# Three rows of an adaLN modulation: from accumulating blocks on VectorE to row products that are summed along the row

## The chip, the cores and the metric

The kernel runs on one core of one Trainium2 chip. What counts is the device time of one execution, in microseconds (us). The kernel before takes 1460.43 us in the median of three runs (1458.61 to 1460.6).

## The reference

One layer of a hybrid diffusion backbone on 256 latent and 256 context tokens of width 2048, everything in float32. Cut to what matters here:

```python
m = silu(c) @ w_mod + b_mod                       # c: 2048 numbers, w_mod: 2048 x 12288
sh1, sc1, g1, sh2, sc2, g2 = split(m, 6)          # six rows of 2048, each (shift, scale, gate) twice
hx = rmsnorm(x, norm1_g) * (1 + sc1) + sh1        # the context tokens go the same way with silu(c_ctx)
z  = hx @ w_in + b_in                             # 2048 x 5648
s5, conv, mlstm = three mixers of z               # state-space scan, convolution, attention-like mLSTM
x  = x + g1 * (concat(s5, conv, mlstm) @ w_out)
hx2 = rmsnorm(x, norm2_g) * (1 + sc2) + sh2
x  = x + g2 * ((silu(hx2 @ wg) * (hx2 @ wu)) @ w_ffn_out)     # inner width 5632
out = rmsnorm(x, norm_f_g)
```

The first two modulation rows (sh1, sc1) are made at the start. The other four, called rows 0 to 3 here (g1, sh2, sc2, g2), are made while the mixers run. g1 is needed in the output projection, sh2 and sc2 behind it at the second norm, and g2 only in the second matrix of the feed-forward.

## The kernel before

Activations lie transposed: 128 features on the partitions, tokens along the free dimension. Every large weight is split into two parts, `whi` and `wlo`, each of a type that TensorE multiplies fast. The weights come as 386 chunks of 128 x 1024, that is eight 128 x 128 tiles, in the order in which TensorE wants them. For each chunk SyncE starts the load into `raw` (`raw_dma`), ScalarE writes `whi` (a cast, L201) and VectorE writes `wlo = raw - whi` (L168). `raw`, `whi` and `wlo` have three buffers each. TensorE (PE) then multiplies with `whi` and `wlo` (L208). So PE can't begin a chunk before VectorE (DVE) has written its `wlo`.

The stages on PE, one after the other: the input projection (first the parts for S5, convolution and keys, then values, queries and the output gate), the gated unit of S5, the output projection in two halves of 16 chunks, then the feed-forward in four blocks. Beside them run jobs: Python generators that the function `pump` steps along by a running estimate of the time on PE (`sc.pe`). These are the convolution (`conv_job`, tile `XB` on DVE), the S5 scan (`s5_job`, tiles `Vr`, `U`, `tmp`), the attention heads (tiles `RH`, `qh`, `dn`) and `mod_job`, which makes the modulation rows 0 to 3. The program that this writes is then put in order once more by the framework's scheduler, for each engine; an instruction that `keep_in_program_order` names keeps its place. Engines work off their queues in order.

`mod_job` before, lines 726 to 764: the weights of the four rows come as 128 loads of 512 KB into four buffers `wm`, which POOL issues (L337, `mod_dma`); a load waits until its buffer has been read. Row 0 is a matrix-vector product on PE, in four column blocks. Rows 1 to 3 are made on DVE: of a block of 512 columns it takes 16 pieces of 128 x 512 and adds up `macc = piece * silu(c) + macc`, with silu(c) as a number for each partition. The first of the 16 is a scaled copy on ScalarE (ACT), the other 15 are `SCALAR_TENSOR_TENSOR` on DVE (L179). The 128 partial sums of each column lie on the partitions then, so PE transposes the block in four pieces (L755) and ACT adds each along the free dimension (L761, a pass and a read of the accumulator). A call `need_mod(q)` steps the job until row q is done: `need_mod(0)` before the output projection, `need_mod(2)` between its halves, `need_mod(3)` before the second matrix of the feed-forward. Row 3 may start only when `go` is 3, which is set in the first block of the feed-forward; the first ACT instruction of each of its blocks keeps its program order.

Of the kernel before, what the change touches and what calls it, by code (L numbers as in the profile page):

```python
# [10 lines left out]
F32 = mybir.dt.float32  # L11
# [8 lines left out]
KT = 16  # L20
# [12 lines left out]
MV_LEAD = 8  # L33
WMQ = 62
MOD_PACE = 3200.0
MOD_PACE_F = 4000.0
MOD_PACE_D = 5000.0
P_CONV, P_S5, P_MOD, P_ATT, P_GATE = (3, 3, 2, 4, 1)
AHEAD, LAG = 3500.0, 500.0
PUMP_EVERY = 8  # L40
# [2 lines left out]
CONV_STEP = 2  # L43
GO_AT = {'k': 2}
LEAD_R, LEAD_S = 2, 1
MOD_PE = {(0, b) for b in range(4)}

# [98 lines left out]


@with_exitstack  # L150
def hybrid_layer_kernel(ctx: ExitStack, tc: tile.TileContext, xt, ctxt, wm1, wmr, wst, wg, bvrow, pvd, cstd, s5p, out):
    nc = tc.nc
    V, S, P, G = nc.vector, nc.scalar, nc.tensor, nc.gpsimd
    sb = ctx.enter_context(tc.tile_pool(name="sb", bufs=1))
# [20 lines left out]
            V.tensor_scalar(o, a, s1, s2, op0=op0, op1=op1)  # L175
        sc.dve += 62 + 0.6 * n_of(o)

    def stt(o, a, s, b, op0, op1):
        V.scalar_tensor_tensor(o, a, s, b, op0=op0, op1=op1)  # L179
        sc.dve += 62 + 1.05 * n_of(o)  # L180

    def vcopy(o, a):
# [11 lines left out]
    def act(o, a, f, bias=0.0, scale=1.0, pin=False):  # L194
        i = S.activation(o, a, f, bias=bias, scale=scale)  # L195
        if pin:
            tc.keep_in_program_order(i)
        sc.act += 190 + 0.84 * n_of(o)
# [24 lines left out]
    def bbank():  # L223
        return bank("b", 3)
# [106 lines left out]
    def wm_dma(key, src, q=None):  # L331
        slot = (4 * key[0] + key[1]) % NWX if len(key) == 2 else 0
        if slot < NWM:
            wm[key] = sb.tile([128, 1024], F32, name="wm", tag="wm", bufs=NWM)
        else:
            wm[key] = wm_extra[slot - NWM]
        i = (q or nc.gpsimd).dma_start(wm[key], src)  # L337
        if q is not None:
            tc.keep_in_program_order(i)
# [33 lines left out]

    plan_pump()

    cs = sb.tile([128, KT, 32], F32, name="cs")
    V.memset(cs, 0.0)
    act(cs[:, :, 0], pvc("c", 0, 16), AF.Silu)
    act(cs[:, :, 1], pvc("cc", 0, 16), AF.Silu)
    b1sc = sb.tile([128, 16], F32, name="b1sc")  # L380
    ts(b1sc, pvc("bm", 16, 16), 1.0, OP.add)

    hx = sb.tile([128, KT, 2, NT], F32R, name="hx", tag="hx")
# [326 lines left out]

    mods = sb.tile([128, 4, 16], F32, name="mods")

    mq = [(q, b, kp) for q in range(4) for b in range(4) for kp in range(8)]
    mst = {"d": 0, "q": 0, "go": 0}

    def phase(n):
# [2 lines left out]
    def mod_dma():  # L719
        if mst["d"] < len(mq):  # L720
            i = mq[mst["d"]]
            wm_dma(i, wmr[i[0], i[1], i[2]])
            mst["d"] += 1

    def mod_job():
      for q in range(4):
        while mst["go"] < q:
            yield 500
        for b in range(4):
            on_pe = (q, b) in MOD_PE  # L730
            acc = sb.tile([128, 512], F32, name="macc", tag="macc", bufs=1)
            if on_pe:
                psm = bbank()
            for kp in range(0, 8, 2):
                w = [wm.pop((q, b, kp + i)).rearrange("p (k n) -> p k n", k=2) for i in range(2)]
                for j in range(4):
                    kt = 2 * kp + j
                    wj = w[j // 2][:, j % 2, :]
                    s = cs[:, kt, 0:1]
                    if on_pe:  # L740
                        mm(psm[32 * j:32 * j + 32, :], cs[:, kt, :], wj, kt < 4, kt >= 12, native=True, tp=(0, 32 * j),
                           pin=j > 0)
                    elif kt == 0:
                        act(acc, wj, AF.Copy, scale=s, pin=q == 3)
                    else:
                        stt(acc, wj, s, acc, OP.mult, OP.add)
                mod_dma()
                mod_dma()
                yield 2 * (MOD_PACE if on_pe else MOD_PACE_D if q < 3 else MOD_PACE_F)
            dst = mods[:, q, 4 * b:4 * b + 4]  # L750
            if on_pe:
                acopy(acc, psm)
            ps = bbank()
            for j in range(4):
                P.transpose(ps[:, 128 * j:128 * j + 128], acc[:, 128 * j:128 * j + 128], ident)  # L755
                sc.pe += 110
            if on_pe:
                rsum(dst, ps.rearrange("p (f j r) -> p f j r", f=4, j=4)[:, :, :, 0])
            else:
                for j in range(4):  # L760
                    S.activation(acc[:, 128 * j:128 * j + 128], ps[:, 128 * j:128 * j + 128], AF.Copy,  # L761
                                    accum_out=dst[:, j:j + 1])
                    sc.act += 390
            tt(dst, dst, pvc("bm", 32 + 16 * q + 4 * b, 4), OP.add)
            yield
        mst["q"] = q + 1

    def need_mod(q):
        mst["go"] = max(mst["go"], q)
# [550 lines left out]
def pack(inp):  # L1320
    f = {k: np.asarray(v) for k, v in inp.items()}

    def cols(v):
        return np.ascontiguousarray(v.reshape(-1, 128).T)

    def feat(x):
        return np.ascontiguousarray(x.T.reshape(KT, 128, NT).transpose(1, 0, 2))

    a = {}
    a["xt"] = feat(f["x"][0])  # L1330
    a["ctxt"] = feat(f["ctx"][0])
    wmod = f["w_mod"][0]
    m1 = wmod[:, :4096].reshape(4, 4, 128, 2, KT, 128)
    a["wm1"] = np.ascontiguousarray(m1.transpose(4, 0, 2, 1, 3, 5)).reshape(KT, 4, 128, 1024)
    mr = wmod[:, 4096:].reshape(8, 2, 128, 4, 4, 512)
    a["wmr"] = np.ascontiguousarray(mr.transpose(3, 4, 0, 2, 1, 5)).reshape(4, 4, 8, 128, 1024)
    mats = {"in": f["w_in"][0][:, :OFF_G], "out": f["w_out"][0], "glu": f["s5_w_glu"][0], "ffi": f["w_ffn_in"][0],
            "ffo": f["w_ffn_out"][0]}
    til = {k: m.reshape(m.shape[0] // 128, 128, m.shape[1] // 128, 128) for k, m in mats.items()}
    w = np.empty((NCH, 128, CH, 128), np.float32)  # L1340
    for i, (m, kt, ct) in enumerate(ORDER):
        w[i // CH, :, i % CH, :] = til[m][kt, :, ct, :]
    a["wst"] = w.reshape(NCH, 128, CH * 128)
    gi = np.array([0, 1, 2, 3, 8, 9, 10, 11, 4, 5, 6, 7, 12, 13, 14, 15])
    g = f["w_in"][0][:, OFF_G:][:, gi]
    a["wg"] = np.ascontiguousarray(g.reshape(KT, 128, 16).transpose(1, 0, 2))
    bi = f["b_in"][0]
    a["bvrow"] = np.ascontiguousarray(bi[None, OFF_V:OFF_O])
    pv = np.zeros((128, NPV + 96), np.float32)

    def put(name, m):
        o, wd = PV[name]
        assert m.shape == (128, wd), (name, m.shape)
        pv[:, o:o + wd] = m

    put("c", cols(f["c"][0]))
    put("cc", cols(f["c_ctx"]))
    put("n1g", cols(f["norm1_g"][0]))
    put("bm", cols(f["b_mod"][0]))
    put("n2g", cols(f["norm2_g"][0]))  # L1360
    put("nfg", cols(f["norm_f_g"]))
    put("bs5", cols(bi[:512]))
    put("bcv", cols(bi[OFF_CONV:OFF_Q]))
    put("bq", cols(bi[OFF_Q:OFF_K]))
    put("bk", cols(bi[OFF_K:OFF_V]))
    put("bo", cols(bi[OFF_O:OFF_G]))
    dw = f["conv_dw_w"][0]
# [12 lines left out]
    put("dcol", np.tile(f["s5_d"][0].reshape(16, 32).T, (4, 1)))  # L1380
    bg = np.zeros((128, 1), np.float32)
    for r in range(4):
        bg[32 * r:32 * r + 4, 0] = bi[OFF_G:][gi[4 * r:4 * r + 4]]
    put("bg", bg)
    a["pvd"] = pv
    cst = np.zeros((128, NCST), np.float32)
    cst[:, C_ID:C_ID + 128] = np.eye(128)
    cst[:, C_MF:C_MF + 128] = np.triu(np.ones((128, 128)))
    cst[:, C_MR:C_MR + 128] = np.tril(np.ones((128, 128)))
    for r in range(32):  # L1390
        q = r % 16
        cst[r, C_SELG + 32 * (q // 4) + q % 4] = 1.0
    cst[:, C_K:C_K + 128] = np.arange(128)
    a["cstd"] = cst
    sp = np.empty((16, 2, 4, 16, 128), np.float32)
    for i, nm in enumerate(("s5_b_re", "s5_b_im")):
        sp[:, :, i] = f[nm][0].reshape(2, 16, 128, 16).transpose(1, 0, 3, 2)
    for i, nm in enumerate(("s5_c_re", "s5_c_im")):
        sp[:, :, 2 + i] = f[nm][0].transpose(0, 1, 3, 2).reshape(2, 16, 128, 16).transpose(1, 0, 3, 2)
    a["s5p"] = np.ascontiguousarray(sp.transpose(0, 4, 1, 2, 3))  # L1400
    return a


_INS = ["xt", "ctxt", "wm1", "wmr", "wst", "wg", "bvrow", "pvd", "cstd", "s5p"]


# [19 lines left out]
```

## Time and profile before

| | |
|---|---|
| median of 3 runs | 1460.43 us |
| the profiled execution | 1461.92 us, of which the span from the first to the last instruction is 1460.2 us |
| PE busy | 1416.0 us, 97% of the span |
| DVE busy | 1058.8 us, 73% |
| ACT busy | 740.4 us, 51% |
| mean granted TensorE clock | 0.99 of full speed |

PE is busy nearly all the time. DVE's share is a mean over stages that differ much, so it has to be read for each stage: the view of windows does that. The view of lines and the timeline give what one instruction costs, and the chain that ended last tells on which instructions the end depends.

### The profile page before, as it was taken

To read this page: it belongs to the slowest core of one execution; us is meant where nothing else is said; L and a number is where in the kernel's file an instruction comes from. 1 tells how busy PE (TensorE), PEld (TensorE's weight loads), DVE (VectorE), ACT (ScalarE), POOL (GpSimd) and SP (SyncE) were. 2 spreads that over 40 slices of the span, in tenths; PEclk is the share of its full clock that TensorE was granted. 3 is DMA by queue.
4 is the path that set the end of the run, shared out by engine and by line. 5 is a ranking of instruction groups with operands and counts; after the bars stand their busy time and mean duration, and the time that the engine had idled before them with its cause. 6 is when DMAs were issued, how large, how long until landed. Compare 5 with 4: busy or idle time off the path is not lost.

```text
span 1460.2 us, 25526 instructions
## 1 busy us (share of the span) xinstructions
PE 1416.0 (97%) x9856; PEld 1242.3 (85%) x9856; DVE 1058.8 (73%) x2104; ACT 740.4 (51%) x1279; POOL 107.3 (7%) x207
## 2 busy tenths in 40 slices
PE   6999899999999999999999999999999999999996
PEld 3888787887878999898998888888888888888885
DVE  7655699998988887888877778566555665556665
ACT  4334786654656555645555545433444334444353
POOL 1221111110001010011000010000000000000000
PEclk9999999999999999999999999999999999999998
DMA  9998464443436666689478787555555555555553
GB/s 365 359 359 300 156 234 142 164 165 117 143 120 226 219 238 236 243 310 343 145 234 278 277 299 240 187 189 186 189 188 187 187 188 188 188 188 188 188 177 112
DMA packets 87929, 315.31 MB, mean 216 GB/s; under 512 B 10096, under 2 KB 10880, under 8 KB 87808
## 3 DMA queue, kind: packets, MB, share of 16 engines
q1 hardware_dynamic: 60912, 216.67, 43.4%
q0 software_dynamic: 26896, 97.02, 18.8%
q8 instruction: 77, 1.26, 0.3%
q14 instruction: 44, 0.36, 0.1%
HBM read 311.55 MB, written 2.10 MB: 215 GB/s over the span
## 4 chain that ended last, share of the span: by engine, by line
PE 87%; DVE 5%; ACT 3%; DMA 2%; issue 1%; SPq 0%; DVEq 0%; ACTq 0%
PE ps_m L208 55%; PE ps_qk L208 20%; PE ps_b L208 12%; DMA raw<-in_wst_dram 1%; DVE tmp L168 1%; ACT whi L201 1%; DVE macc L179 1%; DVE wlo L168 1%; DMA tmp<-in_wg_dram 1%; ACT tmp L195 1%; PE ps_b L845 0%; ACT U L201 0%; PE ps_b L755 0%; DVE tmp L191 0%; DVE tmp L179 0%
## 5 line engine op out<-in xcount | busy, mean ns | idle before, releaser
L168 DVE TENSOR_TENSOR wlo<-raw,whi 128x1024 fp32r<-128x1024 f32 x386 | 471.3, 1222 | 268.0 <-ACT whi L201 264.4
L201 ACT CAST whi<-raw 128x1024 fp32r<-128x1024 f32 x386 | 403.8, 1047 | 478.8 <-PE ps_m L208 240.6
L208 PE MATMUL ps_m<-h,whi 128*128 128x512 f32 (+1 forms) x800 | 251.9, 369 | 3.5 <-ACT h L195 3.5
L208 PE MATMUL ps_m<-ffa,whi 128*128 128x512 f32 x704 | 248.8, 395 | 0.0
L208 PE MATMUL ps_qk<-h,whi 128*128 128x512 f32 (+1 forms) x688 | 233.2, 383 | 0.0
L208 PE MATMUL ps_m<-h,wlo 128*128 128x256 f32 x704 | 199.6, 284 | 0.0
L208 PE MATMUL ps_m<-ffa,wlo 128*128 128x256 f32 x704 | 198.9, 283 | 0.0
L208 PE MATMUL ps_m<-hx,whi 128*128 128x256 f32 x960 | 187.2, 291 | 5.5 <-ACT hx L195 3.6
L208 PE MATMUL ps_qk<-h,wlo 128*128 128x256 f32 x656 | 185.5, 283 | 0.0
L208 PEld LDWEIGHTS ps_m<-h,whi 128*128 128x128 f32 x800 | 144.9, 190 | 30.2 <-ACT h L195 4.0
L208 PEld LDWEIGHTS ps_m<-hx,whi 128*128 128x128 f32 x960 | 149.1, 190 | 24.7 <-issue 16.3
L208 PEld LDWEIGHTS ps_m<-ffa,whi 128*128 128x128 f32 x704 | 132.2, 188 | 32.2 <-issue 1.2
L208 PEld LDWEIGHTS ps_qk<-h,whi 128*128 128x128 f32 x688 | 127.2, 188 | 27.1
L179 DVE SCALAR_TENSOR_TENSOR macc<-wm,cs,macc 128x512 f32<-128x512 f32 x180 | 134.1, 745 | 6.2 <-ACT macc L195 3.8
L208 PE MATMUL ps_m<-hx,wlo 128*128 128x256 f32 x480 | 136.0, 284 | 0.0
L208 PEld LDWEIGHTS ps_m<-h,wlo 128*128 128x128 f32 x704 | 133.1, 189 | 0.0
L208 PEld LDWEIGHTS ps_m<-ffa,wlo 128*128 128x128 f32 x704 | 132.3, 188 | 0.1
L208 PEld LDWEIGHTS ps_qk<-h,wlo 128*128 128x128 f32 x656 | 123.3, 188 | 0.0
L337 POOL DMA_DIRECT2D wm<-in_wmr_dram x128 | 67.5, 528 | 607.7 <-DVE macc L179 431.3
L179 DVE SCALAR_TENSOR_TENSOR xres<-ps_m,mods,xres 128x256 f32<-128x256 f32 x160 | 76.9, 481 | 36.4 <-PE ps_m L208 34.4
L208 PEld LDWEIGHTS ps_m<-hx,wlo 128*128 128x128 f32 x480 | 91.2, 190 | 0.7 <-DVE wlo L168 0.7
L168 DVE TENSOR_TENSOR tmp<-tmp 128x256 f32<-128x256 f32 (+3 forms) x128 | 51.2, 410 | 6.1 <-ACT tmp L195 5.0
(268 smaller groups left out, 2135.7 us busy)
## 6 DMA issues: line engine op xcount, KB each, us to landing
raw<-in_wst_dram SPq DMA_DIRECT2D x386, 512.0 KB, 3.8
wm<-in_wmr_dram POOLq DMA_DIRECT2D x128, 512.0 KB, 5.3
wm<-in_wm_dram POOLq DMA_DIRECT2D x32, 512.0 KB, 7.0
wmu<-in_wm_dram POOLq DMA_DIRECT2D x16, 512.0 KB, 7.0
wmt<-in_wm_dram POOLq DMA_DIRECT2D x7, 512.0 KB, 5.8
wm<-in_wm_dram SPq DMA_DIRECT2D x5, 512.0 KB, 10.3
xr<-in_xt_dram SPq DMA_DIRECT2D x4, 512.0 KB, 6.0
cr<-in_ctxt_dram SPq DMA_DIRECT2D x4, 512.0 KB, 9.0
```

The source lines that it names most:

```text
L168: V.tensor_tensor(out=o, in0=a, in1=b, op=op)
L179: V.scalar_tensor_tensor(o, a, s, b, op0=op0, op1=op1)
L195: i = S.activation(o, a, f, bias=bias, scale=scale)
L201: S.copy(o, a)
L208: i = P.matmul(o, lhsT=l, rhs=r, start=start, stop=stop, skip_group_check=sgc, **kw)
L337: i = (q or nc.gpsimd).dma_start(wm[key], src)
```

## The change

Row 0 stays a product on PE; only its copy goes to a shared buffer `tmp`. For rows 1 to 3 the weights are laid out transposed: the 128 columns of a piece lie on the partitions and 1024 of the 2048 summands along the free dimension, so a piece is 128 x 1024. silu(c) is spread: a load brings half of c (1024 numbers) onto all partitions (`cbr`), and ACT applies silu to it. DVE then multiplies a piece with `cbr` and adds up along the row in one instruction, whose sum (`accum_out`) goes to a column of `mods` or `mpart`. Sixteen pieces and two halves make a row, so 96 products of 128 x 1024 take the place of 180 of 128 x 512 on DVE, 12 scaled copies and 48 passes with 48 reads of the accumulator on ACT, and 48 transposes on PE. The order of the work is rows 1 and 2 with the first half of c, rows 1, 2 and 3 with the second half, and row 3 with the first half again; `cbr` is loaded three times. The pace of the job (`MOD_PACE_R`) is 4700 for a piece. The wait for `go` stands before each product; no instruction of row 3 keeps its program order any more.

```diff
-MOD_PACE_F = 4000.0
-MOD_PACE_D = 5000.0
+MOD_PACE_R = 4700.0
...
-MOD_PE = {(0, b) for b in range(4)}
...
-    def stt(o, a, s, b, op0, op1):
-        V.scalar_tensor_tensor(o, a, s, b, op0=op0, op1=op1)
+    def stt(o, a, s, b, op0, op1, accum=None):
+        V.scalar_tensor_tensor(o, a, s, b, op0=op0, op1=op1, accum_out=accum)
...
-    mq = [(q, b, kp) for q in range(4) for b in range(4) for kp in range(8)]
+    mq = [(0, b, kp) for b in range(4) for kp in range(8)]
+    mq += [(q, hf, i) for hf, qs in ((0, (1, 2)), (1, (1, 2, 3)), (0, (3,))) for q in qs for i in range(KT)]
...
-                    if on_pe:
-                        mm(psm[32 * j:32 * j + 32, :], cs[:, kt, :], wj, kt < 4, kt >= 12, native=True, tp=(0, 32 * j),
-                           pin=j > 0)
-                    elif kt == 0:
-                        act(acc, wj, AF.Copy, scale=s, pin=q == 3)
-                    else:
-                        stt(acc, wj, s, acc, OP.mult, OP.add)
...
-            else:
-                for j in range(4):
-                    S.activation(acc[:, 128 * j:128 * j + 128], ps[:, 128 * j:128 * j + 128], AF.Copy,
-                                    accum_out=dst[:, j:j + 1])
-                    sc.act += 390
...
+        mst["q"] = 1
+        while mst["go"] < 1:
+            yield 500
+
+        at, cbr, part = None, None, None
+        for q, hf, i in mq[32:]:
+            while mst["go"] < q:
+                yield 500
+            if hf != at:
+                at, cbr = hf, sb.tile([128, 1024], F32, name="cbr", tag="cs")
+                nc.gpsimd.dma_start(cbr, crow[0:1, 1024 * hf:1024 * hf + 1024].to_broadcast([128, 1024]))
+                yield 4000
+                act(cbr, cbr, AF.Silu)
+                yield 2000
+            second = hf == (q < 3)
+            if second and i == 0:
+                part = sb.tile([128, KT], F32, name="mpart", tag="b1sc")
+            w = wm.pop((q, hf, i))
+            stt(w, w, 1.0, cbr, OP.mult, OP.mult, part[:, i:i + 1] if second else mods[:, q, i:i + 1])
+            mod_dma()
+            if second and i == KT - 1:
+                tt(part, part, pvc("bm", 32 + 16 * q, KT), OP.add)
+                tt(mods[:, q], mods[:, q], part, OP.add)
+                mst["q"] = q + 1
+            yield MOD_PACE_R
```

What it does to the order is seen on DVE, at two places. The first is the stretch where rows 1 and 2 begin, during the value projection. `macc<-wm,cs,macc` is a product of before, `wm,mods<-wm,cbr` one of the change, `wlo<-raw,whi` the split of a chunk, `XB` belongs to the convolution. Before, ahead of and behind the split of the 47th chunk:

```order
L179 SCALAR_TENSOR_TENSOR tmp<-tmp 128x256
L168 TENSOR_TENSOR wlo<-raw,whi 128x1024
L168 TENSOR_TENSOR tmp<-XB,tmp 128x256
L179 SCALAR_TENSOR_TENSOR macc<-wm,cs,macc 128x512
L168 TENSOR_TENSOR tmp<-XB,tmp 128x256
L179 SCALAR_TENSOR_TENSOR macc<-wm,cs,macc 128x512
L168 TENSOR_TENSOR wlo<-raw,whi 128x1024
```

Now, ahead of and behind the split of the same chunk:

```order
L178 SCALAR_TENSOR_TENSOR XB<-XB,pv 128x256
L178 SCALAR_TENSOR_TENSOR wm,mods<-wm,cbr 128x1024
L178 SCALAR_TENSOR_TENSOR XB<-XB,pv 128x256
L167 TENSOR_TENSOR wlo<-raw,whi 128x1024
L178 SCALAR_TENSOR_TENSOR XB<-XB,pv 128x256
L178 SCALAR_TENSOR_TENSOR wm,mods<-wm,cbr 128x1024
L178 SCALAR_TENSOR_TENSOR XB<-XB,pv 128x256
```

Before, the convolution's products were through at this place; now they stand between the first products of rows 1 and 2. The first of these stands ahead of the split of the 45th chunk, the 24th ahead of that of the 52nd.

The second place is where row 3 begins. Before, this is in the feed-forward (`ffa` is its activation), behind the split of the 140th chunk:

```order
L168 TENSOR_TENSOR wlo<-raw,whi 128x1024 x8
L168 TENSOR_TENSOR tmp<-tmp,ps_m 128x256
L179 SCALAR_TENSOR_TENSOR macc<-wm,cs,macc 128x512
L168 TENSOR_TENSOR ffa<-tmp,ffa 128x256
L168 TENSOR_TENSOR tmp<-tmp,ps_m 128x256
L179 SCALAR_TENSOR_TENSOR macc<-wm,cs,macc 128x512
```

Now row 2 ends with the `mods<-mods,mpart` below, and the two products `wm,mods<-wm,cbr` are the first of row 3, behind the split of the 78th chunk (`wlo`) and among the instructions of an attention head (`RH`, `dn`):

```order
L167 TENSOR_TENSOR wlo<-raw,whi 128x1024
L167 TENSOR_TENSOR RH<-RH,ps_qk 128x512
L167 TENSOR_TENSOR mpart<-mpart,pv 128x16
L178 SCALAR_TENSOR_TENSOR wm,mods<-wm,cbr 128x1024
L174 TENSOR_SCALAR dn<-ps_b,acol 128x1
L167 TENSOR_TENSOR mods<-mods,mpart 128x16
L178 SCALAR_TENSOR_TENSOR wm,mods<-wm,cbr 128x1024
L167 TENSOR_TENSOR dn<-dn,ps_b 128x1
L174 TENSOR_SCALAR dn<-ps_b,acol 128x1
L1104 RECIPROCAL dn<-dn 128x1
L178 SCALAR_TENSOR_TENSOR A_7652<-mods,pv 128x16
```

Row 3 has moved by 62 chunks towards the front. Its last product stands ahead of the split of the 106th chunk, at the end of the first half of the output projection; behind it DVE's queue holds no product of a modulation row.

## Rows read from the trace of the kernel before

**Rows 1.** The page's busy time of each engine.

```profile
PE 1416.0 (97%) x9856; PEld 1242.3 (85%) x9856; DVE 1058.8 (73%) x2104; ACT 740.4 (51%) x1279; POOL 107.3 (7%) x207
```

**Rows 2.** The page's chain that ended last, shares by engine.

```profile
PE 87%; DVE 5%; ACT 3%; DMA 2%; issue 1%; SPq 0%; DVEq 0%; ACTq 0%
```

**Rows 3.** Windows: stretch, length, busy PE, PEld, DVE, ACT, POOL; clock, DMA share, GB/s.

```profile
180.00:340.00 160.00, 157.44 (x1481) 134.11 (x1481) 154.90 (x432) 104.88 (x234) 20.05 (x38) 1.00 0.48 165
361.50:576.50 215.00, 212.78 (x1473) 188.79 (x1472) 180.07 (x437) 126.34 (x269) 19.60 (x37) 0.99 0.57 191
440.00:460.00 20.00, 18.29 (x124) 16.71 (x123) 18.24 (x35) 12.51 (x24) 2.12 (x4) 0.91 0.65 228
640.00:690.00 50.00, 49.92 (x420) 47.87 (x419) 45.77 (x66) 27.53 (x59) 8.45 (x16) 1.00 0.93 332
740.00:905.00 165.00, 164.78 (x955) 144.82 (x954) 131.55 (x183) 87.08 (x150) 14.78 (x28) 1.00 0.80 274
```

**Rows 4.** Timeline, DVE, ahead of the 47th chunk's split: start, length, instruction.

```profile
358.25 0.74 DVE L179 SCALAR_TENSOR_TENSOR macc<-wm,cs,macc 128x512 f32<-128x512 f32 x1
358.91 0.42 DVE L179 SCALAR_TENSOR_TENSOR tmp<-ps_b,tmp 128x256 f32<-128x256 f32 x1
...
360.24 1.22 DVE L168 TENSOR_TENSOR wlo<-raw,whi 128x1024 fp32r<-128x1024 f32 x1
```

**Rows 5.** Timeline, ACT, the 47th chunk's cast.

```profile
357.42 1.03 ACT L201 CAST whi<-raw 128x1024 fp32r<-128x1024 f32 x1
```

**Rows 6.** Timeline, DVE, the 88th chunk's split.

```profile
575.30 1.22 DVE L168 TENSOR_TENSOR wlo<-raw,whi 128x1024 fp32r<-128x1024 f32 x1
```

**Rows 7.** Timeline, PE, its first product with the 88th chunk's `wlo`.

```profile
579.47 0.28 PE L208 MATMUL ps_m<-hx,wlo 128*128 128x256 f32 x1
```

**Rows 8.** Lines by form: count, busy us, mean ns of one, idle time before.

```profile
L179 DVE SCALAR_TENSOR_TENSOR macc<-wm,cs,macc 128x512 f32<-128x512 f32 x180 | 134.1, 745 | 6.2 <-ACT macc L195 3.8 <-DMA wm<-in_wmr_dram 1.0
L179 DVE SCALAR_TENSOR_TENSOR XB<-XB,pv 128x256 f32<-128x256 f32 x120 | 53.6, 477 | 0.6
L195 ACT ACT_TABLE_LOAD x25 | 32.1, 1283 | 3.7 <-DMA pv<-in_pvd_dram 3.3
L761 ACT ACTIVATION_READ_ACCUMULATOR macc<-ps_b 128x1 f32 x48 | 10.1, 210 | 0.0
L337 POOL DMA_DIRECT2D wm<-in_wmr_dram x128 | 67.5, 528 | 607.7 <-DVE macc L179 431.3 <-PE ps_b L208 112.6 <-DVE RH L175 36.8
```

**Rows 9.** Chain that ended last, in order of time: start, length (three of twelve groups).

```profile
640.09 0.44 PE ps_b L755 x4
...
789.49 0.44 PE ps_b L755 x4
...
925.63 0.44 PE ps_b L755 x4
```

**Rows 10.** DMA issues: count, KB each, median us from issue to landing.

```profile
wm<-in_wmr_dram POOLq DMA_DIRECT2D x128, 512.0 KB, 5.3
...
bvb<-in_bvrow_dram SPq DMA_DIRECT2D x2, 256.0 KB, 3.6
```

**Rows 11.** The same loads (L337) from 620 to 690 us alone.

```profile
DMA to landing us min/median/max: 4.8/5.8/7.5
```

**Rows 12.** Waits of PE for the splits: engine, line, for whom, us, times, longest.

```profile
PE ps_m L208 <- DVE wlo L168: 0.6, 1, 0.6
...
PE ps_b L208 <- DVE wlo L168: 0.2, 1, 0.2
```

More of the change, by code (lines that the diff above doesn't have):

```diff
@@ L150, in hybrid_layer_kernel @@
 @with_exitstack
-def hybrid_layer_kernel(ctx: ExitStack, tc: tile.TileContext, xt, ctxt, wm1, wmr, wst, wg, bvrow, pvd, cstd, s5p, out):
+def hybrid_layer_kernel(ctx: ExitStack, tc: tile.TileContext, xt, ctxt, wm1, wmg, wmr, wst, wg, bvrow, crow, pvd, cstd,
+                        s5p, out):
     nc = tc.nc
@@ L374, in hybrid_layer_kernel @@
     plan_pump()
-    cs = sb.tile([128, KT, 32], F32, name="cs")
+    cs = sb.tile([128, KT, 32], F32, name="cs", tag="cs")
     V.memset(cs, 0.0)
@@ L379, in hybrid_layer_kernel @@
     act(cs[:, :, 1], pvc("cc", 0, 16), AF.Silu)
[L380 removed]
+    b1sc = sb.tile([128, 16], F32, name="b1sc", tag="b1sc")
     ts(b1sc, pvc("bm", 16, 16), 1.0, OP.add)
@@ L721, in mod_dma @@
             i = mq[mst["d"]]
-            wm_dma(i, wmr[i[0], i[1], i[2]])
+            wm_dma(i, wmg[i[1], i[2]] if i[0] == 0 else wmr[i[0] - 1, i[2], i[1]])
             mst["d"] += 1
     def mod_job():
-      for q in range(4):
-        while mst["go"] < q:
-            yield 500
         for b in range(4):
-            on_pe = (q, b) in MOD_PE
-            acc = sb.tile([128, 512], F32, name="macc", tag="macc", bufs=1)
-            if on_pe:
-                psm = bbank()
+            psm = bbank()
             for kp in range(0, 8, 2):
-                w = [wm.pop((q, b, kp + i)).rearrange("p (k n) -> p k n", k=2) for i in range(2)]
+                w = [wm.pop((0, b, kp + i)).rearrange("p (k n) -> p k n", k=2) for i in range(2)]
                 for j in range(4):
                     kt = 2 * kp + j
-                    wj = w[j // 2][:, j % 2, :]
-                    s = cs[:, kt, 0:1]
-                    if on_pe:
-                        mm(psm[32 * j:32 * j + 32, :], cs[:, kt, :], wj, kt < 4, kt >= 12, native=True, tp=(0, 32 * j),
-                           pin=j > 0)
-                    elif kt == 0:
-                        act(acc, wj, AF.Copy, scale=s, pin=q == 3)
-                    else:
-                        stt(acc, wj, s, acc, OP.mult, OP.add)
+                    mm(psm[32 * j:32 * j + 32, :], cs[:, kt, :], w[j // 2][:, j % 2, :], kt < 4, kt >= 12, native=True,
+                       tp=(0, 32 * j), pin=j > 0)
                 mod_dma()
                 mod_dma()
[L749 to L752, printed above, removed]
+                yield 2 * MOD_PACE
+            acc = tmp()
+            acopy(acc, psm)
             ps = bbank()
@@ L756, in mod_job @@
                 sc.pe += 110
-            if on_pe:
-                rsum(dst, ps.rearrange("p (f j r) -> p f j r", f=4, j=4)[:, :, :, 0])
-            else:
-                for j in range(4):
-                    S.activation(acc[:, 128 * j:128 * j + 128], ps[:, 128 * j:128 * j + 128], AF.Copy,
-                                    accum_out=dst[:, j:j + 1])
-                    sc.act += 390
-            tt(dst, dst, pvc("bm", 32 + 16 * q + 4 * b, 4), OP.add)
-            yield
-        mst["q"] = q + 1
+            dst = mods[:, 0, 4 * b:4 * b + 4]
+            rsum(dst, ps.rearrange("p (f j r) -> p f j r", f=4, j=4)[:, :, :, 0])
+            tt(dst, dst, pvc("bm", 32 + 4 * b, 4), OP.add)
+            yield
+        mst["q"] = 1
[22 more added lines that the diff above has]
+            yield MOD_PACE_R
     def need_mod(q):
@@ L1334, in pack @@
     a["wm1"] = np.ascontiguousarray(m1.transpose(4, 0, 2, 1, 3, 5)).reshape(KT, 4, 128, 1024)
-    mr = wmod[:, 4096:].reshape(8, 2, 128, 4, 4, 512)
-    a["wmr"] = np.ascontiguousarray(mr.transpose(3, 4, 0, 2, 1, 5)).reshape(4, 4, 8, 128, 1024)
+    mg = wmod[:, 4096:6144].reshape(8, 2, 128, 4, 512)
+    a["wmg"] = np.ascontiguousarray(mg.transpose(3, 0, 2, 1, 4)).reshape(4, 8, 128, 1024)
+    a["wmr"] = np.ascontiguousarray(wmod[:, 6144:].T.reshape(3, KT, 128, 2, 1024).transpose(0, 1, 3, 2, 4))
+    a["crow"] = np.ascontiguousarray(f["c"][0:1])
     mats = {"in": f["w_in"][0][:, :OFF_G], "out": f["w_out"][0], "glu": f["s5_w_glu"][0], "ffi": f["w_ffn_in"][0],
@@ L1401, in pack @@
     return a
-_INS = ["xt", "ctxt", "wm1", "wmr", "wst", "wg", "bvrow", "pvd", "cstd", "s5p"]
+_INS = ["xt", "ctxt", "wm1", "wmg", "wmr", "wst", "wg", "bvrow", "crow", "pvd", "cstd", "s5p"]
 def kernel(**inputs):
```

## The prediction

> **What bounds the kernel now.** I read the page's busy times first, then the chain that ended last, then windows stage by stage. PE is busy 97% of the span [rows 1] and is 87% of the chain [rows 2]: whatever takes a matmul away or makes PE wait moves the end one for one, and work on another engine is free until PE waits for it. PE waits for DVE wherever the split of a chunk (`wlo`) is late, so the second thing to read is how full DVE is in each stage. From 180 to 340 us DVE is busy 154.9 of 160 us, 97%, and PE still 157.4: this is DVE as full as it gets here, with the S5 and convolution jobs. From 361.5 to 576.5 us DVE is busy 180.1 of 215 us, so 34.9 us are free. From 640 to 690 it has 4.2 us left of 50, and in the feed-forward from 740 to 905, where row 3 lies, 33 us of 165 [rows 3]. So a DVE load that is moved out of the feed-forward into the middle of the kernel goes from where it costs nothing to where there is little room.
>
> **What goes on PE.** Twelve groups of four transposes, 0.44 us each on the chain [rows 9]: 5.3 us in all. The four groups of row 1 lie in the stretch that DVE will set, below, and buy nothing there; the eight of rows 2 and 3 are in PE-bound stretches: -3.5 us. ACT loses 60 instructions and their reads and gets three silu passes, with table loads of 1.28 us [rows 8]; at 126 of 215 us busy [rows 3] it hides that.
>
> **What one new product costs on DVE.** No product of 1024 with a sum stands in the trace. The nearest rows: with 512 elements the present product takes 745 ns, a product of 256 takes 477 [rows 8], so 1.047 ns per element, and 745 + 536 = 1281 ns for 1024. An instruction right behind another starts before the other's end: the product at 358.25, 0.74 long, is followed at 358.91 [rows 4], so 0.08 us are shared and a product in a dense queue costs 1.20, an old one 0.66 to 0.75; I take 0.69. To fetch the sum may cost a second instruction. On ACT that read takes 210 ns [rows 8]; nothing to 0.21 are my ends, and I take 0.10, since small DVE instructions share their ends as well. So 1.30 us for a product, between 1.20 and 1.41.
>
> [...]
>
> **What the new order asks of DVE.** The order shows two things. The 96 products all stand ahead of the 106th chunk's split; row 3, which before ran in the feed-forward, follows row 2 at once. And rows 1 and 2 start with a burst: 24 products between the 45th and the 52nd split, with the rest of the convolution between them. I compare DVE's work between the 47th split and the 88th, which before ends at 361.5 and 576.5 us [rows 4, 6]. I counted both orders.
> - Out: 64 old products, 64 x 0.69 = 44.2 us.
> - In: 73 new ones, 73 x 1.30 = 94.9 us (the last 16 are of row 3).
> - In: 14 shorter ones that stood ahead of the 47th split before, ten of them the convolution's: about 5 us.
> - Off: some 25 splits that now follow another instruction directly, 0.08 each: 2 us.
> So DVE has 94.9 + 5 - 44.2 - 2 = 53.7 us more to do. It has room for 34.9 (its idle time there), plus 1.8 (the 47th cast ends at 358.45 [rows 5], and DVE took it up only at 360.24 [rows 4]), plus 3.0 (PE first uses the 88th `wlo` at 579.47 [rows 7], its split ended at 576.52): 39.7 us. PE comes to the 88th chunk 53.7 - 39.7 = 14.0 us later, with DVE never idle. The 97% of rows 3 is the best that a stage shows, so I add 3% of 234 us: 7 us. From there on DVE has no more lag to add: only 16 products are left, among splits of the output projection, and behind the 106th split DVE is nearly free. PE can't make up what it lost, since it is full to the end.
>
> **The rest.** [...] POOL's loads: each of the four `wm` buffers is refilled when its product is done, and landing takes 5.3 us in the median [rows 10]. With the product (1.3) and POOL's issue (0.53 [rows 8]) that is (5.3 + 1.8) / 4 = 1.8 us per product, and DVE's own spacing in the burst is (24 x 1.30 + 17 x 0.40 + 7 x 1.14) / 24 = 1.9: just covered. At a landing of 7.5 [rows 11] it is 2.3, which over 24 products is 10 us. Behind a load that waits stand the small loads of S5, so S5 would be late as well. I take 3 us, with 0 and 10 as the ends. The three loads of `cbr` resemble that of `bvb`, which lands in 3.6 us [rows 10]; the third silu stands in ACT's queue just ahead of a cast, so a late load there holds the cast back: within these 3 us.
>
> **The sum**, against the profiled execution of 1461.9 us: + 14.0 (DVE full) + 7 (not quite full) + 1.7 (clock) + 3 (loads) - 3.5 (transposes) = +22.2, so 1484.1 us. The profiled execution lies 1.5 us above the median of the runs: 1483 us.
>
> The ends: with 1.20 per product the sum is 7.3 smaller, with no idle time another 7, with no late load and no slow clock 4.7: 22.2 - 19 = +3, 1463. With 1.41 it is 8 larger, with DVE idle as in a stage that waits back and forth (say 8% instead of 3) 12 more, with loads at their upper end 7, with the second slow stretch 2: +51, 1512.
>
> **The rivals.**
> - *DVE catches up and only PE's transposes count* (faster). The place is the same stretch, and the point is 39.7 us of room: if a product costs 1.05 us, its elements alone, the new products are 76.7 and DVE's extra work is 35.5, under the room. Then PE never waits more than now, all 5.3 us of transposes are saved, and ACT is freer at the second norm: about 1455 us. Against it: every row of DVE has a fixed part on top of its elements, 0.13 us at the least when dense (0.66 for 512).
> [...]
> - *The loads are the bound in the burst.* (7.5 + 1.8) / 4 = 2.3 us for a product in the whole run to the 88th chunk is less than DVE's spacing there (234 / 73 = 3.2), so this can hold only for the first 24: +10 instead of 3, and S5 late behind it in POOL's queue by as much again: 1500. This lies inside the range.
> - *Row 3 stays behind the output projection*, as the wait for `go` asks. Then 16 products, 21 us, leave the stretch, DVE needs 33 us more and has 39.7: 1457. The order speaks against it: it is what the engines work off.
>
> **Chances.** Forecast and the loads together, that is slower by 3 to 51 us: 0.80. DVE catches up: 0.08. Half the rate: 0.06. Row 3 in the feed-forward: 0.02. Something between forecast and no change: 0.04. A difference of 0.2% (2.9 us) is what a measurement can tell from none. Faster by more: 0.08; within it: 0.05; slower: 0.87. Range 1463 to 1512.
>
> **What the profile will show.** [...] DVE over 95% busy from about 360 to 590 us, where it was 84%. Among PE's waits a large new one on `wlo` (0.8 us in all now [rows 12]), spread over many chunks between the 51st and the 106th, 15 to 25 us in sum, and the granted clock below 1.00 in those windows. The feed-forward without any DVE product, and as long as before but for 1.8 us. If DVE shows idle time in the middle and PE waits for nothing new, I am wrong on the load; if PE waits for DVE and DVE for `wm`, it is POOL's loads.

## The result, and the profile after

The changed kernel takes 1476.59 us (median of four runs, 1473.82 to 1480.2) against 1460.01 (1458.61 to 1460.6): a ratio of 1.0116, 95% interval 1.0092 to 1.0141, or 16.6 us slower. The profiled execution of after is the fastest of its four, 1473.82 us with a span of 1472.1; that of before lies above its median. So the two traces differ by 11.9 us, and the trace shows that much of the 16.6.

The page's busy times and the chain of after answer to [rows 1, 2]:

```profile
PE 1415.2 (96%) x9808; PEld 1242.2 (84%) x9808; DVE 1044.2 (71%) x2110; ACT 723.5 (49%) x1176; POOL 109.2 (7%) x210
...
PE 78%; issue 9%; DVE 6%; ACT 3%; POOL 2%; DMA 2%; SPq 0%; POOLq 0%; DVEq 0%; ACTq 0%
```

DVE is 14.6 us less busy in the whole and PE is slower all the same. Where the work lies decides. The same five windows as [rows 3], with three more (columns as there):

```profile
180.00:340.00 160.00, 157.77 (x1476) 134.85 (x1476) 155.22 (x429) 105.66 (x233) 20.36 (x39) 1.00 0.50 173
361.50:576.50 215.00, 203.74 (x1370) 177.97 (x1370) 201.52 (x501) 116.46 (x232) 36.60 (x69) 0.96 0.75 265
440.00:460.00 20.00, 20.00 (x165) 18.05 (x164) 19.36 (x43) 13.14 (x24) 1.32 (x3) 1.00 0.51 165
640.00:690.00 50.00, 50.00 (x428) 48.91 (x427) 33.63 (x46) 21.18 (x29) 0.53 (x1) 1.00 0.61 207
740.00:905.00 165.00, 165.00 (x991) 146.84 (x990) 91.76 (x116) 79.67 (x118) 0.00 (x0) 1.00 0.55 187
380.00:385.00 5.00, 0.04 (x1) 0.00 (x0) 5.00 (x13) 2.01 (x4) 1.59 (x3) 0.85 0.95 363
385.00:395.00 10.00, 7.46 (x54) 5.65 (x54) 8.78 (x25) 5.89 (x16) 1.06 (x2) 0.50 0.49 184
590.00:620.00 30.00, 23.19 (x171) 22.22 (x170) 23.19 (x45) 18.57 (x28) 2.65 (x5) 0.93 0.66 236
```

From 361.5 to 576.5 us DVE has gone from 180.1 to 201.5 busy and PE from 212.8 to 203.7. In the feed-forward DVE has gone from 131.6 to 91.8: there it has room that nobody asked for. PE's loss stands in two short windows, 380 to 395 and 590 to 620. Its waits from 340 to 660 us (us in total, times, longest), to be read beside [rows 12]:

```profile
PE ps_b L741 <- ACT tmp L200: 6.7, 1, 6.7
PE ps_m L207 <- ACT RH L194: 3.4, 1, 3.4
PE ps_m L207 <- ACT mixm L200: 1.9, 1, 1.9
...
PE ps_m L207 <- DVE wlo L167: 0.9, 1, 0.9
```

The waits on `wlo` are what they were. One wait of 6.7 us is new. On ACT's timeline (start, length, instruction, in brackets the idle time ahead and what ended it) the instruction that PE waits for is the `COPY tmp<-ps_b` of row 0's last group:

```profile
378.93 0.60 ACT L194 ACTIVATE tmp<-tmp,pv 128x256 f32<-128x256 f32 x1 [1.19 <-DVE tmp L167]
...
383.71 0.60 ACT L194 ACTIVATE tmp<-tmp,pv 128x256 f32<-128x256 f32 x1 [2.26 <-DVE tmp L167]
...
386.08 0.56 ACT L200 COPY tmp<-ps_b 128x512 f32<-128x512 f32 x1
```

It stands behind the convolution's norm, and the norm waits for DVE, which does this at that time:

```profile
380.30 1.22 DVE L178 SCALAR_TENSOR_TENSOR wm<-wm,cbr 128x1024 f32<-128x1024 f32 x1
381.44 0.08 DVE L178 DVE_READ_ACCUMULATOR wm<-wm,cbr 128x1 f32 x1
381.44 0.42 DVE L167 TENSOR_TENSOR mixc<-tmp,mixc 128x256 fp32r<-128x256 f32 x1
381.78 1.22 DVE L178 SCALAR_TENSOR_TENSOR wm<-wm,cbr 128x1024 f32<-128x1024 f32 x1
```

Between any two small instructions that the norm needs stands a product of 1.22. PE then stood still (0.04 us busy from 380 to 385), and the clock that was granted was 0.50 from 385 to 395 us. The second place is at 595 us: ACT waits for the third load of the spread row, then does its silu, and only then what PE waits for:

```profile
595.57 1.28 ACT L194 ACT_TABLE_LOAD   x1 [3.01 <-DMA cbr<-in_crow_dram]
596.86 1.06 ACT L194 ACTIVATE cbr<-cbr 128x1024 f32<-128x1024 f32 x1
597.82 0.46 ACT L194 ACTIVATE RH<-ps_m,pv 128x256 f32<-128x256 f32 x1
```

How late PE is, chunk by chunk, is the best map. The table gives the time at which PE's first matmul with a chunk's `wlo` starts in the profiled execution, less the same time in before (us). The last column is the profiled execution's time less the median of all runs of that kernel (before: 1.9). Chunks are counted from 1, as in the prediction; the expectations quoted below mostly count them from 0, so their 84th to 96th is the 85th to 97th here.

| run | 49th | 53rd | 67th | 89th | 95th | 105th | 141st | last | less median |
|---|---|---|---|---|---|---|---|---|---|
| after | -6.2 | 7.0 | 9.8 | 9.9 | 15.8 | 16.0 | 13.7 | 11.9 | -2.8 |
| own_buffer | -0.2 | 1.9 | -0.1 | 5.6 | 9.3 | 9.3 | 13.1 | 11.2 | 1.7 |
| spread_start | -1.8 | 1.0 | -4.4 | 5.9 | 10.3 | 10.3 | 28.2 | 26.4 | 2.8 |
| row3_held | -5.3 | 7.5 | 10.1 | 9.6 | 7.0 | 7.0 | 4.6 | 2.7 | -1.5 |
| two_loads | -4.2 | 9.1 | 10.8 | 11.6 | 17.4 | 17.4 | 16.3 | 14.4 | -0.1 |
| both_edits | -0.6 | 1.5 | -2.3 | 1.7 | 0.5 | -0.6 | -2.3 | -4.2 | -2.5 |
| paced | 1.3 | 5.6 | 0.1 | -0.2 | -0.1 | -0.2 | -1.9 | -3.0 | 0.1 |
| fixed_order_half | -0.3 | 1.7 | 1.2 | 1.6 | 8.2 | 8.2 | 6.2 | 3.6 | -4.6 |
| placed_half_two_loads | 1.2 | 5.6 | 5.7 | 7.6 | 8.6 | 8.6 | 7.4 | 5.6 | 2.1 |

One execution's steps are not exact: up to the 66th split the order on DVE and the cost of a product are the same in the last two runs of the table, and they stand 3.9 us apart at the 53rd.

The lead of 6.2 at the 49th in after is work put off: row 0's last transposes come at 386.7 us, in before at 354. What counts is the 53rd: 7.0 us. Then come 2.8 to the 67th, nothing from there to the 89th, 5.9 between the 89th and the 95th, and from the 105th to the end 4.1 come back.

My theory at this point had two places: the late copy at the 49th to 53rd chunk, and the third load of the spread row at the 89th to 95th. The rival was the prediction's own: DVE is full, and a delay taken away at one place comes back at another.

### The profile page after: what moved, and what is told of

It reads as the page before. It is cut to its first block, busy times and chain, and to the rows that moved or that the text cites. A ratio compares the mean times of both kernels' runs of the same rounds, so it can differ in the third digit from the quotient of the medians.

```text
span 1472.1 us, 25253 instructions
## 1 busy us (share of the span) xinstructions
PE 1415.2 (96%) x9808; PEld 1242.2 (84%) x9808; DVE 1044.2 (71%) x2110; ACT 723.5 (49%) x1176; POOL 109.2 (7%) x210
## 4 chain that ended last, share of the span: by engine, by line
PE 78%; issue 9%; DVE 6%; ACT 3%; POOL 2%; DMA 2%; SPq 0%; POOLq 0%; DVEq 0%; ACTq 0%
PE ps_m L207 50%; PE ps_qk L207 18%; PE ps_b L207 10%; POOL wm L336 2%; DVE tmp L167 1%; DVE wm L178 1%; DMA tmp<-in_wg_dram 1%; DMA cbr<-in_crow_dram 0%; ACT tmp L194 0%; DVE XB L178 0%; DVE wlo L167 0%; ACT U L200 0%; ACT gT L200 0%; PE ps_b L850 0%; DVE tmp L178 0%
## 5 line engine op out<-in xcount | busy, mean ns | idle before, releaser
L178 DVE SCALAR_TENSOR_TENSOR wm<-wm,cbr 128x1024 f32<-128x1024 f32 x96 | 116.2, 1217 | 7.2 <-ACT cbr L194 4.3
L336 POOL DMA_DIRECT2D wm<-in_wmr_dram x96 | 50.9, 530 | 261.6 <-DVE wm L178 187.3
## 6 DMA issues: line engine op xcount, KB each, us to landing
wm<-in_wm_dram SPq DMA_DIRECT2D x5, 512.0 KB, 10.3
```

The source lines that it names most:

```text
L178: V.scalar_tensor_tensor(o, a, s, b, op0=op0, op1=op1, accum_out=accum)
```

## Experiments

Each was timed in several rounds beside the kernel before, whose median lay between 1459.50 and 1460.42 us; the ratio is to before, with its 95% interval.

**own_buffer.**

```
-    cs = sb.tile([128, KT, 32], F32, name="cs", tag="cs")
+    csb = sb.tile([128, 1024], F32, name="cs", tag="cs")
+    cs = csb[:, 0:512].rearrange("p (k n) -> p k n", k=KT)
...
-            acc = tmp()
+            acc = csb[:, 512:1024]
```

> Edit: row 0's copy gets a buffer of its own (the unused half of the silu(c) buffer) in place of one of the four shared ones, and so the spread row of rows 1 and 2 is loaded only behind row 0's last transposes: their first products stand ahead of the 47th split, 10 of them ahead of the 53rd instead of 26. Theory (one place): the step of 13 us between the 48th and the 52nd chunk is a wait of PE for row 0's copy, which stands behind the convolution's norm, which stands among the products on DVE, and the half clock behind it. Then PE's wait on that copy (6.7 us) is gone, no half-clock stretch at 382 to 396 us, and the time is 13 us less than that of the changed kernel: 1463 to 1466. Rival (DVE is full): the products only move back, DVE is late for as much at other chunks, waits on wlo grow by 8 us or more, and the time stays at 1473 to 1479.

Measured: 1471.49 us, 1.0086 (1.0070 to 1.0102), 5.1 us less than after. Between theory and rival. The wait for the copy is gone and PE is on time up to the 67th chunk. Then the loss comes in again, a little at a time and not on `wlo`:

```profile
PE ps_b L207 <- DVE RH L167: 4.2, 3, 2.8
PE ps_m L207 <- DVE vx L167: 2.9, 1, 2.9
PE ps_m L207 <- ACT whi L200: 2.4, 1, 2.4
PE ps_m L207 <- DVE xres L178: 2.4, 2, 1.7
...
PE ps_m L207 <- DVE wlo L167: 1.2, 2, 0.7
```

Three of the four largest are on DVE's short instructions: attention's `RH`, the value projection's `vx`, the residual's `xres`. The splits are made ahead and have a reserve; results without a reserve are late.

**spread_start.**

```
-            stt(w, w, 1.0, cbr, OP.mult, OP.mult, part[:, i:i + 1] if second else mods[:, q, i:i + 1])
+            stt(w, w, 1.0, cbr, OP.mult, OP.mult, part[:, i:i + 1] if second else mods[:, q, i:i + 1], pin=q < 3 and hf == 0)
```

(`pin` is a new argument of `stt`: it keeps the instruction in the program's order.)

> Edit: the 32 products of the first halves of rows 1 and 2 are held at the program's pace (about one for each chunk from the 47th on) instead of 24 in a burst; row 0's copy keeps its shared buffer. Everything behind moves back too: row 3 then lies between the 112th and the 144th split. Theory (one place): with one product instead of two or three between two instructions of the convolution's norm the copy is about 5 us earlier, PE's wait for it falls from 6.7 to under 2 us, and the time to 1462 to 1468. Rival (the shared buffer alone is the cause, the burst not): the wait stays at 5 to 7 us and the time at 1471 to 1477. Rival (DVE is full): new waits on wlo behind the 84th chunk, 1473 to 1480.

Measured: 1485.47 us, 1.0180 (1.0161 to 1.0198), 8.9 us more than after. The early part went as the theory said: no wait for the copy of 0.6 us or more, and 4.4 us ahead of before at the 67th chunk, so it was the burst that made the copy late. What was put off lands where DVE has no room, and there it is `wlo`, from 600 to 680 us:

```profile
PE ps_m L209 <- DVE wlo L167: 6.4, 2, 5.5
PE ps_qk L209 <- ACT tmp L196: 3.2, 2, 2.5
```

**row3_held.** The same line with `pin=q == 3`.

> Edit: the 32 products of row 3 are really held back until the feed-forward (they stand between the 140th and the 205th split). Theory (two places): the step at the 48th to 52nd chunk stays as it is; the loss of 5 to 6 us between the 84th and the 96th chunk, where the third load of the spread row and its silu stand in ACT's queue ahead of a cast, is gone: 1468 to 1473. Rival (the row that stands too early is the whole loss): 1457 to 1462. Rival (that row costs nothing where it is): 1475 to 1478.

Measured: 1466.12 us, 1.0046 (1.0031 to 1.0062), 10.5 us less than after: more than expected. PE loses nothing from the 89th to the 105th and wins 2.6. Row 3 in the feed-forward is free, as its windows show (580 to 610 us, where PE is now busy 29.2 of 30, and the feed-forward):

```profile
580.00:610.00 30.00, 29.16 (x240) 28.30 (x239) 18.71 (x34) 20.23 (x31) 0.00 (x0) 1.00 0.47 148
740.00:905.00 165.00, 165.00 (x967) 145.70 (x966) 122.96 (x174) 83.12 (x123) 14.78 (x28) 1.00 0.81 272
```

The edit takes away two things at that place, row 3's products and the third load. The next run takes away one.

**two_loads.**

```
-    mq += [(q, hf, i) for hf, qs in ((0, (1, 2)), (1, (1, 2, 3)), (0, (3,))) for q in qs for i in range(KT)]
+    mq += [(q, hf, i) for hf in range(2) for q in (1, 2, 3) for i in range(KT)]
...
-            second = hf == (q < 3)
+            second = hf == 1
```

(and the wait for `go` ends at 2 for row 3 too.)

> Edit: row 3's first half is made with the first half of the spread row, together with rows 1 and 2, and its second half with theirs, so that the spread row is loaded twice instead of three times. The number of products and their place as a whole (ahead of the 104th split) stay. Theory (two places): the loss between the 84th and the 96th chunk comes from the third load and its silu: 1469 to 1473. Rival (it comes from DVE's load of products there, which is the same): 1475 to 1479.

Measured: 1476.46 us, 1.0114 (1.0097 to 1.0132): nothing gained. The delay between the 89th and the 95th is 5.8 us as before. ACT no longer waits for a load, but DVE is 27.5 of 30 us busy there, with more products in this window than after had, and PE waits for its `xres` (first the window, then PE's waits from 575 to 620 us):

```profile
590.00:620.00 30.00, 23.56 (x170) 22.13 (x169) 27.45 (x53) 15.97 (x27) 4.22 (x8) 0.91 0.76 282
```

```profile
PE ps_m L207 <- DVE xres L178: 2.7, 1, 2.7
PE ps_m L207 <- ACT RH L194: 1.3, 1, 1.3
```

My theory of the second place fell, in this form. Three of the last runs come back to it.

**half_products.**

```
-            stt(w, w, 1.0, cbr, OP.mult, ...
+            stt(w[:, 0:512], w[:, 0:512], 1.0, cbr[:, 0:512], OP.mult, ...
```

> Edit: each of the 96 products works on 512 of its 1024 columns only, so that half of each modulation sum of rows 1 to 3 is left out; loads, table loads and the three loads of the spread row stay. DVE then has about 52 us less to do ahead of the 106th split. Theory (DVE is full there, and whichever of its results PE needs next is late): nearly all of the loss goes, PE's waits behind the 52nd chunk are as before, and the time is 1455 to 1462; what may stay is the wait for row 0's copy. Rival (the discrete places, that is the shared buffer, the loads of wm and of the spread row, are the loss by themselves): 1468 to 1476.

Measured: 1473.9 us, 1.0094 (1.0079 to 1.0108). It looks like a verdict for the rival and is none. The order changed with the price: the last product now stands ahead of the 81st split instead of the 106th. The products ran into their loads. First DVE's longest waits from 361.5 to 600 us, then the window of 460 to 540 us, with the DMA share at 0.98:

```profile
DVE wm L178 <- DMA wm<-in_wmr_dram: 24.5, 20, 3.7
```

```profile
460.00:540.00 80.00, 72.26 (x458) 64.25 (x459) 62.62 (x184) 35.77 (x62) 19.54 (x37) 0.96 0.98 366
```

After itself waits 2.8 us for these loads in the same stretch.

**both_edits.** own_buffer and row3_held together.

> Edit: row 0's copy in its own buffer, and row 3 held back until the feed-forward. Theory (DVE is full): with 16 products fewer ahead of the 88th split DVE needs some 33 us more than before against a room of 39.7, and the early wait is gone too: 1458 to 1463. Rival (the two effects are the same loss seen at two places, and the second edit buys nothing on top of the first): 1464 to 1468.

Measured: 1460.21 us, 1.0007 (0.9995 to 1.0018): no different from before. 16.4 us less than after, where the single effects add up to 15.6. They are two losses, not one seen twice. PE still waits for `RH` and `vx` as in own_buffer (from 340 to 660 us), and the time is that of before, so these two waits alone are not what own_buffer lost:

```profile
PE ps_b L209 <- DVE RH L167: 4.4, 4, 1.7
PE ps_m L209 <- DVE vx L167: 3.0, 1, 3.0
```

**paced.** As both_edits, with `pin=True` for all products and

```
-MOD_PACE_R = 4700.0
+MOD_PACE_R = 2200.0
```

> Edit: as both_edits, and the products of rows 1 and 2 are held at the program's pace as well, with a shorter pace: one or two for each chunk from the 47th to the 98th, never three, and row 3 between the 140th and the 174th. Theory (DVE is full where products come in bursts, and has room for them when they are spread to the 98th chunk, since the new form costs 1.15 to 1.3 us where two old products cost 1.38): 1454 to 1459, faster than before. Rival (spreading buys nothing once row 3 is held): as both_edits, 1459 to 1465.

Measured: 1458.81 us, 1.0000 (0.9990 to 1.0009): not faster than before, and 1.4 below both_edits, less than can be told apart. This is the best version that I found.

**paced_shared.** paced with `acc = tmp()` again.

> Edit: as paced, but with row 0's copy in one of the four shared buffers, as the change has it. It tells what the shared buffer costs by itself where no burst of products stands among the convolution's norm. Theory (it is the burst that makes the copy late): PE's wait for it is under 3 us, time within 3 us of paced. Rival (the shared buffer alone): a wait of 5 to 7 us and a half-clock stretch, 6 to 13 us above paced.

Measured: 1459.76 us, 1.0002 (0.9990 to 1.0015). Within 1 us of paced, and PE doesn't wait for the copy at all. So the shared buffer costs nothing unless a burst of products stands in the norm. A buffer of its own with the burst left in was not tried: own_buffer puts it in the spread row's place, and so puts the burst off as well.

**fixed_order, fixed_order_half, placed_full, placed_half_two_loads.** These should separate price from order: every product is held at a place by a table of counts per chunk, which is that of after but for four or five of the first 24. The edit also leaves out the two pauses of the job behind the load of the spread row and behind its silu.

```
+        if i == 0 and c >= 30:
+            mst["cap"] += TAB.get(c + 2, 0)
+            while mst["n"] < mst["cap"]:
+                sc.step(mj)
```

> Edit: none of the arithmetic; each product is held at a place given by a table, namely the one that it has in the changed kernel (the count of products between two splits is the same but for four or five of the first 24, which stand one split later). A control for fixed_order_half: both theories expect the time of the changed kernel, 1473 to 1480; row 0's copy, which stands behind slightly fewer products, may come some 2 us earlier.

> Edit: as fixed_order, and each product works on 512 of its 1024 columns, so that half of each modulation sum of rows 1 to 3 is left out. In half_products the cheaper products moved forward and packed closer, until DVE waited 24.5 us for their loads; here their places are kept. DVE has about 51 us less to do in the same order with the same loads. Theory (what the changed kernel lost is DVE's time for the products): 1456 to 1464. Rival (the loss is the places where the products stand, so that DVE waits for loads and for ACT in front of what PE needs): 1468 to 1476.

Measured: fixed_order 1537.71 us, 1.0523 (1.0509 to 1.0536), no control at all. The program's pacing counts the products as DVE's time, and so put attention off; PE ran 15 us ahead of before and then lost nearly 100 waiting for it. fixed_order_half 1470.14 us, 1.0062 (1.0049 to 1.0075), is the useful one: from the 55th split to the 106th DVE's other instructions stand where they stand in after, but for 16 ahead of the 60th and up to ten around the 75th to 80th. Ahead of the splits of the 51st to the 53rd, 20 to 54 of them stand earlier than in after. PE is 1.6 us late at the 89th chunk where after is 9.9, though DVE waits 10.7 us for `wm` from 361.5 to 600 us (2.8 in after). Of these 8.3 us, 5.3 are there at the 53rd already, where the order is not that of after; behind it after loses 2.9 to the 89th and this run nothing. Then 6.6 us are lost at the second place, and here PE waits behind the load (ACT's waits from 575 to 600 us, PE's from 575 to 620). The pause that is gone brings the silu nearer to its load, so that ACT waits 4.8 us for it where it waits 3.0 in after:

```profile
ACT L197 <- DMA cbr<-in_crow_dram: 4.8, 1, 4.8
...
PE ps_m L210 <- ACT RH L197: 4.4, 1, 4.4
```

> Edit: as fixed_order (the products at the places of the changed kernel, by a table), but the program's pacing counts the products for nothing, so that attention and S5 are not pushed back by them as in fixed_order; from the 62nd split on the other instructions of DVE stand as in the changed kernel. None of the arithmetic is changed. It is the control that fixed_order failed to be: both theories expect the time of the changed kernel, 1472 to 1481. If it is far above, the comparison of fixed_order_half with the changed kernel has to go by the changed kernel alone.

> Edit: as fixed_order_half (products over 512 of 1024 columns, half of each sum of rows 1 to 3 left out, same places), and the spread row is loaded twice instead of three times. In fixed_order_half ACT stood 4.8 us at 586 us before the third load, and PE waited 4.4 us behind it. Theory (with DVE's time out of the way the third load is what is left): 1460 to 1465, that is 5 to 10 us less than fixed_order_half, and less than 2 us of delay at the 94th chunk. Rival (the load only hides another wait of the same size, as it did in two_loads): 1467 to 1472.

Measured: placed_full 1494.38 us, 1.0253 (1.0227 to 1.0279), no control either: it loses 32.9 us by the 53rd chunk, where S5's steps now stand behind the products. Behind that it wins 4.7 to the 67th and loses 1.8 to the 89th and 4.1 to the 95th, where after loses 2.8, 0.1 and 5.9. So fixed_order_half can be held against after alone. placed_half_two_loads 1465.42 us, 1.0035 (1.0023 to 1.0048), 4.7 us less than fixed_order_half in the median. From the 89th to the 95th 1.0 us is lost instead of 6.6, and the wait of 4.4 is gone. But PE comes to the 89th 6.0 us later in it, and at the 95th the two are level (8.6 and 8.2): these two traces do not show the gain of the medians.

The second place thus has two limits. With the load gone and DVE full, 5.8 us are lost (two_loads, with three products more from 590 to 620 us than after has). With DVE relieved and the load there, 6.6. With both relieved, 2.6 are won (row3_held, which comes to the 89th as late as after); the 1.0 of placed_half_two_loads points the same way. What each limit would cost by itself in after is not shown.

## Why the prediction was right, and where not

**Direction and size.** In the medians +16.6 us were measured, and 1476.59 lies in the range. The sum of +22.2 was made against the profiled execution, and there it is +11.9: what stood in it as 21.0 for DVE and 1.7 for the clock came as 9.9 up to the 89th chunk, the 3 for the loads as 6.1 from there to the 105th, the transposes' -3.5 as -4.1. The direction was reasoned; that the time lies so near is in part luck, since the largest term was twice too high and came about in another way.

**Price of a product.** 1.217 us and a read of the sum of 0.082 behind it, 1.30 together. That this is the forecast's number is chance: it had 1.281 for the product, and took off a shared end.

```profile
L178 DVE SCALAR_TENSOR_TENSOR wm<-wm,cbr 128x1024 f32<-128x1024 f32 x96 | 116.2, 1217 | 7.2 <-ACT cbr L194 4.3 <-DMA wm<-in_wmr_dram 2.8
```

How they follow each other on DVE's timeline:

```profile
368.44 0.08 DVE L178 DVE_READ_ACCUMULATOR wm<-wm,cbr 128x1 f32 x1
368.44 1.22 DVE L178 SCALAR_TENSOR_TENSOR wm<-wm,cbr 128x1024 f32<-128x1024 f32 x1
369.58 0.08 DVE L178 DVE_READ_ACCUMULATOR wm<-wm,cbr 128x1 f32 x1
369.58 1.22 DVE L178 SCALAR_TENSOR_TENSOR wm<-wm,cbr 128x1024 f32<-128x1024 f32 x1
```

As a cost in a full queue it was 0.16 too dear: the next instruction starts with the read, and from start to start are 1.14 us. Over 73 products that is 11 us of the forecast's 94.9. Half the rate, to which the prediction gives a chance of 0.06, did not come: at twice its 1.047 ns per element 1024 would take 2.1 us, by an estimate, and 1.217 were measured. Where a source lies made little difference to a product of 256. With one source in PSUM, `ps_m`, it took 481 ns in before, and `XB<-XB,pv`, which reads two from SBUF, took 477 [rows 8]:

```profile
L179 DVE SCALAR_TENSOR_TENSOR xres<-ps_m,mods,xres 128x256 f32<-128x256 f32 x160 | 76.9, 481 | 36.4 <-PE ps_m L208 34.4
```

**DVE's budget from the 47th to the 88th split.** Forecast: 53.7 us more work, 39.7 of room, 7 lost to idle time, so PE 21.0 late. Here are the windows between the ends of the two splits in before, after, row3_held and both_edits (columns as in [rows 3]):

```profile
361.46:576.51 215.05, 212.83 (x1474) 188.84 (x1472) 180.12 (x437) 126.39 (x269) 19.60 (x37) 0.99 0.57 191
352.50:588.55 236.05, 224.79 (x1508) 197.03 (x1508) 220.47 (x535) 124.95 (x242) 41.16 (x78) 0.96 0.76 267
353.40:585.53 232.13, 221.43 (x1485) 194.16 (x1485) 205.53 (x502) 124.60 (x241) 32.22 (x61) 0.96 0.70 239
358.28:579.32 221.04, 213.38 (x1479) 189.59 (x1478) 207.03 (x502) 123.17 (x238) 35.93 (x68) 1.00 0.74 260
```

From before to after the stretch grew by 21.0 us, DVE's work by 40.3 (against 53.7; the price of the product is 11 of the difference), and its idle time fell from 34.9 to 15.6 (forecast: to 7). The stretch began 9.0 us earlier, and 2.2 of PE's reserve at the 88th went: 21.0 - 9.0 - 2.2 = 9.8, PE's delay there. Work too high by 13.4 and idle time too low by 8.6: the two errors partly cancel. But the stretch is not one account, as the forecast took it. 7.0 of the delay are there at the 53rd chunk. In row3_held DVE works 15 us less in it, and PE is 9.6 late at the 89th, as in after. In both_edits DVE is as full as in after, 94% to 93%, and PE is 1.7 late. Idle time of DVE behind the burst does not give back what a wait inside it cost.

**The step that failed** is "a large new one on `wlo` ..., spread over many chunks". PE waits 0.9 us for `wlo` in the longest such wait, and 1.1 in all from 340 to 660 us. DVE's queue was nearly as full as forecast (93% between the two splits, over 95 forecast), but its splits are made ahead, and other results, with no reserve, were late: first the convolution's norm, and behind it, over ACT, row 0's copy, for which PE waits 6.7 us. I had read the burst and priced its loads, and did not ask what small instructions it stands between. That the burst makes the copy late is shown by spread_start and paced_shared, where the copy has its shared buffer and PE does not wait for it. Whether a burst of cheaper products at the same places would do so is open: fixed_order_half (1.6 instead of 9.9 us late at the 89th) speaks against it, but its order is another ahead of the 55th split, and placed_half_two_loads, with the same cheap products, is 7.6 late there.

**"From there on DVE has no more lag to add"** behind the 88th chunk failed too: 5.9 us between the 89th and the 95th. The 16 products that were left stand among the gated mixes and the first output projection, and the third load, which I had put "within these 3 us", stands at the same place: PE's longest wait there, 3.4 us, is behind its silu.

**Row 3 hoisted.** The order was right against the words of the change, and it was worth 10.5 us by itself, the largest part that one edit moved.

**Transposes**: 3.5 forecast for eight groups; between the 105th and the end 4.1 come back, four steps of 0.44 of them in the feed-forward.

**Clock**: the sum has +1.7 for one slow stretch, and its upper end 2 more for a second. Before has a stretch below full clock in one window of [rows 3], from 440 to 460 us; that a new wait would bring one at the price of 1.7 is shown by no run. What the runs showed in its place differs from wait to wait. In after, from the end of the wait of 6.7 us, PE works 9.66 us at a granted clock of 0.50, which by an estimate from this row is 4.8 us lost:

```profile
386.70:397.20 10.50, 9.66 (x63) 7.75 (x64) 7.08 (x21) 5.15 (x15) 1.06 (x2) 0.50 0.47 156
```

In both_edits PE waits 3.0 us for `vx` at 441 us, and the granted clock stays at 1.00:

```profile
436.00:458.00 22.00, 19.03 (x139) 17.66 (x138) 20.25 (x40) 18.88 (x34) 2.64 (x5) 1.00 0.62 210
```

**Loads as the bound in the burst.** Not in after (DVE waits 2.8 us for `wm`); half_products, where products cost half and move closer, is that rival come true.

What stays open: of the 13.2 us that PE loses from the 49th to the 53rd chunk, 6.7 are the wait and some 4.8 the clock, and the rest is not assigned. The medians differ by 4.7 us more than the profiled executions. The three other runs of after show a mean granted clock of 0.981 to 0.982 where the profiled one has 0.985; by an estimate 0.003 of 1475 us is 4.4 us, so more time at the lower clock may be the cause, but no trace shows where.

## What to carry to other kernels

Work moved onto an engine that has a reserve in one place (the splits) shows up where the same engine has none: list the short instructions that the new long ones will stand between, and who waits for each. Where a pin goes with the instruction that carried it, the row it held moves, whatever the text says; read the order, and pin again. An edit that removes one of two limits at the same place can measure as zero, so a null result clears a suspect only when the other limit is out of the way; and an experiment that makes an instruction cheaper may also move it.

## What the runs showed of the hardware that was not expected

The sum of a product on DVE is fetched by an instruction of its own (82 ns in the mean of 96 in after), but the next product starts with it, 1.14 us after the one before, so in a full queue the read adds nothing to these 1.14 us. The spread row's three loads of 512 KB on POOL's queue landed as follows (smallest, median and largest):

```profile
DMA to landing us min/median/max: 5.3/5.6/7.3
```

That is near the 5.3 us of the `wm` loads of the same size in [rows 10], and more than the 3.6 of `bvb` there, which has half the bytes and goes by SP's queue. Which part the size has in that and which the queue is not shown.
